# Layer 0's second FFN product by seven quarter products, with conditioning work and late norms placed elsewhere

## The chip, the cores and the metric

One core of one Trainium2 chip runs the whole program. The metric is the device time of one execution in microseconds, of the kernel before the median of three runs. TensorE (PE) multiplies; VectorE (DVE), ScalarE (ACT) and GpSimd (POOL) do the rest; SyncE (SP) issues the loads, in program order.

## What is computed

A decoder trunk of two layers for 512 tokens of width 1024, in float32. Layer 0 mixes tokens with a gated MLP in chunks of 128, layer 1 with attention over 16 heads whose logits carry a forget gate; each is followed by a SwiGLU FFN with 2816 hidden columns. Shift, scale and gate of every norm come from a conditioning vector `c`.

```python
mod = c_act @ ada_w[layer] + ada_b[layer]
sh_m, sc_m, g_m, sh_f, sc_f, g_f = jnp.split(mod, 6, axis=-1)
h = modulate(rms_norm(x, pre_mix_g[layer]), sh_m, sc_m)
y = gmlp_mixer(h, ...) if layer < N_A_LAYERS else fox_mixer(h, ...)
x = x + g_m[:, None, :] * rms_norm(y, post_mix_g[layer])
h = modulate(rms_norm(x, pre_ffn_g[layer]), sh_f, sc_f)
g, u = jnp.split(h @ w_gu, 2, axis=-1)
y = (jax.nn.silu(g) * u) @ w_down
x = x + g_f[:, None, :] * rms_norm(y, post_ffn_g[layer])
```

After layer 0 keys, values and forget gates are projected from `x` under a modulation of their own (kv). The mixer of layer 0 takes `z = gelu(h @ w_in)`, halves `u` and `v`, normalises `v`, multiplies it by `w_s` over each chunk and by `u`, and ends with `w_out`.

## The kernel before

Every product is made of three with operands split into a high part (`whi`, rounded by ACT) and a rest (`wlo`, by DVE): high by high, high by rest, rest by high (`moving`, L298 to L300; `prods`, L535; `prod`, L411 to L413). `load_split` (L109) loads a piece of weights of 128x1024 into one of three `raw` buffers and splits it; the loads stand on SP in program order, and each waits until its buffer is free.

The stages follow one another on PE: `v` and then `u` columns of `w_in` in eight chunks (`zchunk`), `w_s` and the first half of `w_out` for 16 groups (`spatial`, `ytrans`, `wout0`), the second half of `w_out` (`moving` with a tail of five held pieces), layer 0's gate and up products (`ffn`, 22 steps `m`), its second product `w_down`, then vf (value and forget-gate columns), k, q, attention, `w_o`, and layer 1's FFN. Four row blocks of 128 tokens, `n` = 0 to 3, have their own PSUM banks.

At a stage's end `boundary` takes each row block: `residual` (L333) sums squares on ACT (`sumsq`, L325), multiplies by the gate row (`y`, L341), adds to `x` (L347) and sums squares of the new `x`; `xrs` makes the reciprocal root; `prenorm_half` (L266) then scales two row blocks to `xr` (ACT, L263), transposes them on PE (`ps_x`, L275) and writes `hT` (L250 to L257, with `keep` copies at vf).

The conditioning vector's products are done on DVE in blocks: `ada_block` (L179) loads 128x1024 of `ada_w` and reduces it against `c` (L182). Closures for the blocks stand in a list `bg`, from which `run_bg` takes some at fixed places in the program; within the FFNs each uses the single buffer `rawb`, elsewhere one of the three `raw`. Behind the last block of a kind a `fin` finishes its columns or its gate row.

Layer 0's second product is `moving` over two column halves and 22 row pieces: 2 x 22 x 4 x 3 = 528 products of 128x512. Layer 1's is `down` (L360): Strassen-Winograd over the quarters of weights and hidden values, seven products for eight, 462. It needs sums of hidden quarters (`sums`, L556, POOL) and of weight quarters, which `weight_sums` (L489) makes on DVE during the gate/up stage and stores to a scratch `td` in HBM.

The order on each engine is set by a scheduler from the program's order and from priorities: `boundary` runs under `high_priority`, `issue_after` and `behind_norm` hold instructions behind others, and `pin` keeps attention's instructions in the written order. In attention `ORDER` (L53) is a string of tokens per head: `score` (L1100 to L1105: products, minimum on DVE, exponential on ACT), transposes, values, and between them fillers. `headnorm` gives k and q their norms: squares on ACT, reductions on DVE (L976), one reciprocal root (`rsqrt`, L139), multiplications.

## Time and profile before

| | |
|---|---|
| median of 3 runs | 1352.62 us (1349.98 to 1353.37) |
| the profiled execution | 1356.19 us, of which its span 1354.2 |
| mean granted TensorE clock | 0.995 |
| PE busy | 1319.9 us, 97% |
| DVE, ACT, POOL busy | 870.5, 580.4, 221.3 us |
| DMA | 221.08 MB, mean 163 GB/s |

A span is from the first instruction to the last. PE's products are pipelined, so its busy time is the time in which some product was under way; an idle time in brackets is a real stop. A row of a timeline names the engine, the line, what is written from what, and the wait before it with the engine that ended it.

### The profile page before, as it was taken

The page shows a single profiled execution, that of the slowest core. Times are in us where ns is not written, and L with a number is a line of the kernel's source. Part 1 is how long each engine was busy: PE and PEld are TensorE (multiplying, and loading weights), DVE is VectorE, ACT ScalarE, POOL GpSimd, SP SyncE. Part 2 cuts the span into 40 slices and gives each one's busy share as a digit, 9 for nine tenths or more (in the row PEclk, how much of TensorE's full clock was granted, in tenths as well). Part 3 has the DMA queues.
Part 4 walks back from the last instruction along what each step waited for, and adds up shares of the span by engine and source line. Part 5 has one row for each costly group of instructions (what it writes and reads, how often), then busy time and mean ns, then how long its engine had stood idle before and what let it go on. Part 6 is the DMA issues. An engine that isn't in the chain of part 4 may idle for free.

```text
span 1354.2 us, 17576 instructions
## 1 busy us (share of the span) xinstructions
PE 1319.9 (97%) x6376; PEld 1102.7 (81%) x6376; DVE 870.5 (64%) x1572; ACT 580.4 (43%) x995; POOL 221.3 (16%) x216
## 2 busy tenths in 40 slices
PE   7999999999999999999999998999999999999997
PEld 5888888779888888787889886887799888888886
DVE  6869858656455555554564766888675554536688
ACT  6524433345232223112562536887552222224665
POOL 0000000012111111000020405675021221212000
PEclk9999999999999999999999998999999999999999
DMA  9564446733666666674232331111336767665663
GB/s 368 187 225 133 132 125 203 267 105 125 204 214 188 192 197 203 207 257 125 87 119 78 95 106 47 38 35 33 109 110 207 253 207 259 197 199 173 199 191 129
DMA packets 71336, 221.08 MB, mean 163 GB/s; under 512 B 8657, under 2 KB 8913, under 8 KB 71250
## 3 DMA queue, kind: packets, MB, share of 16 engines
q1 hardware_dynamic: 70674, 218.92, 50.4%
q8 instruction: 50, 0.82, 0.3%
q10 hardware_dynamic: 576, 1.05, 0.2%
q14 instruction: 36, 0.29, 0.1%
HBM read 206.03 MB, written 13.65 MB: 162 GB/s over the span
## 4 chain that ended last, share of the span: by engine, by line
PE 64%; DMA 5%; DVE 5%; ACT 2%; issue 1%; DVEq 0%; ACTq 0%
PE acc L535 33%; PE acc L298 4%; PE acc L299 4%; PE acc L300 4%; DMA rawb<-in_ada_t 4%; PE acc L1048 3%; PE acc L1135 1%; PE acc L1259 1%; PE ps_x L412 1%; PE ps_x L411 1%; PE ps_x L413 1%; PE acc L1260 1%; PE acc L1261 1%; PE acc L412 1%; PE acc L411 1%
## 5 line engine op out<-in xcount | busy, mean ns | idle before, releaser
L535 PE MATMUL acc<-hT,whi 128*128 128x512 f32 (+1 forms) x1600 | 425.0, 364 | 0.0
L116 ACT ACTIVATE whi<-raw 128x1024 fp32r<-128x1024 f32 (+2 forms) x190 | 197.6, 1042 | 452.1 <-PE acc L535 169.1
L120 DVE TENSOR_TENSOR wlo<-raw,whi 128x1024 fp32r<-128x1024 f32 (+2 forms) x190 | 229.1, 1209 | 170.0 <-ACT whi L116 168.5
L535 PEld LDWEIGHTS acc<-hT,whi 128*128 128x128 f32 x1600 | 276.1, 189 | 47.4
L535 PE MATMUL acc<-hT,wlo 128*128 128x512 f32 (+1 forms) x800 | 263.6, 364 | 0.0
L535 PEld LDWEIGHTS acc<-hT,wlo 128*128 128x128 f32 x800 | 138.8, 189 | 23.7
L299 PE MATMUL acc<-wlo,hT 128*128 128x512 f32 (+1 forms) x352 | 135.0, 384 | 0.0
L300 PE MATMUL acc<-whi,hT 128*128 128x512 f32 (+1 forms) x352 | 134.8, 383 | 0.0
L298 PE MATMUL acc<-whi,hT 128*128 128x512 f32 (+1 forms) x352 | 134.5, 383 | 0.0
L182 DVE CUSTOM_DVE_ANT_0 rawb<-rawb,c_bc 128x1024 f32<-128x1024 f32 x59 | 77.1, 1307 | 83.9 <-DMA rawb<-in_ada_t 61.0
L299 PEld LDWEIGHTS acc<-wlo,hT 128*128 128x128 f32 x352 | 66.1, 188 | 12.7 <-DVE wlo L120 0.3
L298 PEld LDWEIGHTS acc<-whi,hT 128*128 128x128 f32 x352 | 66.1, 188 | 12.5
L300 PEld LDWEIGHTS acc<-whi,hT 128*128 128x128 f32 x352 | 66.1, 188 | 12.4
L257 POOL TENSOR_TENSOR hT<-hfull,hT 128x256 fp32r<-128x256 f32 x36 | 29.2, 819 | 277.7 <-DVE hT L256 154.8
L550 POOL TENSOR_TENSOR hid<-sg,hid 128x512 fp32r<-128x512 f32 (+1 forms) x25 | 36.7, 1471 | 193.5 <-ACT hid L549 193.5
L299 PE MATMUL acc<-wlo,hid 128*128 128x512 f32 x144 | 56.7, 394 | 4.5 <-DVE wlo L120 4.5
L182 DVE CUSTOM_DVE_ANT_0 raw<-raw,c_bc 128x1024 f32<-128x1024 f32 x37 | 45.1, 1220 | 20.8 <-DMA raw<-in_ada_t 20.6
L298 PE MATMUL acc<-whi,hid 128*128 128x512 f32 x144 | 56.1, 391 | 0.6 <-ACT junk L325 0.6
L300 PE MATMUL acc<-whi,hid 128*128 128x512 f32 x144 | 56.2, 390 | 0.0
L390 DVE TENSOR_TENSOR hT<-raw,hT 128x512 fp32r<-128x512 f32 x69 | 46.2, 702 | 13.1 <-ACT hT L389 12.9
L389 ACT ACTIVATE hT<-raw 128x512 fp32r<-128x512 f32 x69 | 42.0, 625 | 18.1 <-PE ps_x L412 7.1
L541 ACT ACTIVATE sg<-acc 128x512 f32<-128x512 f32 (+1 forms) x50 | 26.6, 536 | 52.1 <-PE acc L535 50.8
(336 smaller groups left out, 2370.0 us busy)
## 6 DMA issues: line engine op xcount, KB each, us to landing
raw<-in_w_gu SPq DMA_DIRECT2D x88, 512.0 KB
raw<-in_ada_t SPq DMA_DIRECT2D x53, 512.0 KB
raw<-in_w_down SPq DMA_DIRECT2D x44, 512.0 KB
rawb<-in_ada_t SPq DMA_DIRECT2D x43, 512.0 KB
raw<-in_w_in SPq DMA_DIRECT2D x32, 512.0 KB
raw<-td SPq DMA_DIRECT2D x44, 256.0 KB
raw<-in_w_down SPq DMA_DIRECT2D x33, 256.0 KB
raw<-in_w_out SPq DMA_DIRECT2D x16, 512.0 KB
```

Of the source, the lines that this page charges most:

```text
L116: ACT(hi[:, :width], raw[:, :width], AF.Copy)
L120: lo_eng.tensor_tensor(lo[:, :width], raw[:, :width], f32(hi[:, :width]), sub)
L182: nc.vector.tensor_tensor_reduce(raw, raw, c_bc, 1.0, 0.0, mul, add, dst)
L257: last = lo_eng.tensor_tensor(lo, full, f32(hi), sub)
L298: MM(banks[n], lh, wh, start=kt == 0, stop=False)
L299: MM(banks[n], lh, wl, start=False, stop=False)
L300: MM(banks[n], ll, wh, start=False, stop=kt == kts - 1)
L389: ACT(hi, w, AF.Copy)
L390: TT(lo, w, f32(hi), sub)
L535: MM(o, (hi, hi, lo)[z][:, ks], h[z == 1][kt][:, cs], start=i == 0, stop=i == 3 * KT - 1)
L550: nc.gpsimd.tensor_tensor(hid[1][m][:, cs], sg, f32(hid[0][m][:, cs]), sub)
L1048: pin(MM(box[0], (hi, hi, lo)[z][:, cs], h[z == 1][kt], start=kt + z == 0, stop=kt == KT - 1 and z == 2))
```

## The change

Layer 0's FFN takes the form of layer 1's: weight sums during its gate/up stage, `down` after it, the hidden values no longer split. `weight_sums` stores three pieces for four, and `down` makes the fourth, `t1`, again from the weights it loads; the store is put behind the next step. `down` has its own pool in both layers.

The blocks of `bg` are taken elsewhere: 12 in the last two `u` chunks, 14 in `wout0` (two for each pair of groups but the last), none before the second half of `w_out` and 6 (kv) in its tail, 28 in layer 0's gate/up stage (54 before), only a finish in its `down`, 24 in vf, k and q, where none stood before. The number of blocks is the same, 112 loads in all.

`lnorm` takes two operations for three. `prenorm_half` becomes a generator that transposes one row block, then the other; of a stage's second half it is held, and `next_late` lets it go on behind named products of the next stage. vf takes rows 2 and 3 first, which `down` finishes first. The reductions of the second half of q stand behind heads' scores (tokens B and C of head 0), its root and multiplications in pair 1.

```diff
-        for kp in range(KT // 2):
-            ps = aux.tile([P, 2, 256], F32, name="ps_x", tag="ps_s" if kp % 2 else "ps_t")
+        tr = [aux.tile([P, 2, 256], F32, name="ps_x", ...) for kp in range(KT // 2)]
+        yield
+        for kp in range(KT // 2):
+            turn(kp, 0)
+        yield
...
-        for i in range(NP):
-            r0 = halves(src[0, i, :, :512], td[i][:, 0])
-            r1 = halves(td[i][:, 1], td[i][:, 2])
+            b11, b12 = halves(src[0, i, :, :512], src[1, i, :, :512])
+            r1 = halves(td[i][:, 0], td[i][:, 1])
+            t1 = small.tile([P, S], F32, name="t1", tag="t2", bufs=3)
+            TT(t1, b12, b11, sub)
...
+                sums_at = dict(zip((4, 5, 7, 8, 10, 11, 13, 14, 16, 17, 19), range(NF // 2)))
...
-                                run_bg(1 if layer else 1 + j)
+                                run_bg(1 if layer or j == 0 or m % 3 == 0 or m > 15 else 0)
...
-                moving([w_down[layer, 0, i] for i in range(NF // 2)], NF, 512, lhs, first_half(y0, ss, row))
-                moving([w_down[layer, 1, i] for i in range(NF // 2)], NF, 512, lhs,
+                down(w_down[layer], td, qa, qb, fp, fd, row, done)
...
-                with tc.issue_after(ylast[0].ins):
-                    run_bg(2)
+                if g < 14:
+                    with tc.issue_after(ylast[0].ins):
+                        run_bg(2)
...
-               extra=lambda i: load_x(xp) if i == 2 else None)
+               extra=lambda i: load_x(xp) if i == 2 else None, n_bg=0, tail_bg=(3, 3, 0, 0))
...
-            for grp in ((0, 1), (2, 3)):
+            for grp in ((2, 3), (0, 1)):
...
+                        if kt == (3 if j else KT - 1):
+                            next_late(mm)
...
+                elif tok in "BC" and i == 0:
+                    for n in range(2 * "BC".index(tok), 2 * "BC".index(tok) + 2):
+                        later[n]()
+                elif tok == "C" and p_ == 1:
+                    close(0)
+                    later["end"]()
```

Three places in the order. First DVE at the end of w_out: `wlo` is a weight split (of w_out, then of gate/up weights), `y1` the first residual's product with the gate row. Before:

```order
L120 TENSOR_TENSOR wlo_2242<-raw_2238,whi_2240 128x1024
L120 TENSOR_TENSOR wlo_2622<-raw_2618,whi_2620 128x1024
L120 TENSOR_TENSOR wlo_2628<-raw_2624,whi_2626 128x1024
L341 TENSOR_TENSOR y1_2276<-acc_2118,grow_1600 128x512
L162 SCALAR_TENSOR_TENSOR rq_0_2279<-ss_565 128x1
```

Now (the rows that only read a block's sum out, 128x1, are left out):

```order
L120 TENSOR_TENSOR wlo_2253<-raw_2249,whi_2251 128x1024
L182 ISA raw_2255,A_kv_2121<-raw_2255,c_bc_75 128x1024
L182 ISA raw_2258,A_kv_2121<-raw_2258,c_bc_75 128x1024
L182 ISA raw_2261,A_kv_2121<-raw_2261,c_bc_75 128x1024
L182 ISA raw_2321,A_kv_2121<-raw_2321,c_bc_75 128x1024
L182 ISA raw_2324,A_kv_2121<-raw_2324,c_bc_75 128x1024
L182 ISA raw_2327,A_kv_2121<-raw_2327,c_bc_75 128x1024
L349 TENSOR_TENSOR y1_2296<-acc_2129,grow_1246 128x512
L162 SCALAR_TENSOR_TENSOR rq_0_2299<-ss_565 128x1
L120 TENSOR_TENSOR wlo_2608<-raw_2604,whi_2606 128x1024
L165 RECIPROCAL rpost_2297<-rq_1_2300 128x1
```

Six blocks stand between the last w_out split and the residual, and a gate/up split stands inside the residual's chain.

Second ACT at the change from the second FFN product to vf: the first `whi` of 128x704 in each list is vf's third piece, `x` the residual stream by row block (before, `x_2186` is block 2, and block 3 follows; now `x_2193` is block 0 and `x_2195` block 1, the last), `keep` and `hfull` belong to the prenorm. Before:

```order
L325 ACTIVATE junk,sx_2611<-x_2186 128x512
L163 ACTIVATE rq_5303<-rq_5302 128x1
L325 ACTIVATE junk,ss<-acc 128x512
L280 COPY keep_5186<-ps_x 128x2x256
L116 ACTIVATE whi<-raw 128x704
L163 ACTIVATE rq_5352<-rq_5351 128x1
L116 ACTIVATE whi<-raw 128x704
L263 ACTIVATE xr<-x_2186,rst_2610 128x1024
```

Now:

```order
L250 ACTIVATE hfull<-ps_x,B_kv,A_kv 128x256
L287 COPY keep_5636<-ps_x 128x2x256
L263 ACTIVATE xr<-x_2193,rst_2585 128x1024
L287 COPY keep_5637<-ps_x 128x2x256
L333 ACTIVATE junk,ss<-u_5138 128x512
L333 ACTIVATE junk,ss<-acc 128x512
L163 ACTIVATE rq_5787<-rq_5786 128x1
L333 ACTIVATE junk,sx_2586<-x_2195 128x512
L116 ACTIVATE whi<-raw 128x704
L333 ACTIVATE junk,sx_2586<-x_2195 128x512
L116 ACTIVATE whi<-raw 128x704
```

vf's third piece stood ahead of the last row block's residual; now it stands behind that residual, and behind the prenorm of the half that was finished first.

Third DVE at the start of attention: `mn` are score minima (`pr0` to `pr3` by row block; the first group is head 0's last, the other head 1's), `s8` the reductions of q, `rs` and `r8` the root. Before, with steps of the root left out:

```order
L1104 ISA pr3_6627,mn_6628<-ps_s_6624,mask_6289 128x512
L976 TENSOR_REDUCE s8_5919<-sqt_6637 128x8
L976 TENSOR_REDUCE s8_5919<-sqt_6647 128x8
L976 TENSOR_REDUCE s8_5919<-sqt_6657 128x8
L976 TENSOR_REDUCE s8_5919<-sqt_6667 128x8
L143 TENSOR_SCALAR rs_0_6671<-s8_5919 128x32
L146 TENSOR_SCALAR r8_5920<-rs_0_6671 128x32
L153 SCALAR_TENSOR_TENSOR rs_1_6672<-rs_1_6672,rs_0_6671 128x32
L154 SCALAR_TENSOR_TENSOR r8_5920<-rs_1_6672,r8_5920 128x32
L1104 ISA pr0_6697,mn_6698<-ps_s_6694,mask_6289 128x128
```

Now, with read-outs and four operations of the values' path left out:

```order
L1142 ISA pr0_7189,mn_7190<-ps_s_7186,mask_6781 128x128
L1142 ISA pr1_7196,mn_7197<-ps_s_7193,mask_6781 128x256
L1142 ISA pr2_7203,mn_7204<-ps_s_7200,mask_6781 128x384
L1142 ISA pr3_7213,mn_7214<-ps_s_7210,mask_6781 128x512
L1009 TENSOR_REDUCE s8_6387<-sqt_7147 128x8
L1009 TENSOR_REDUCE s8_6387<-sqt_7156 128x8
L1161 TENSOR_TENSOR pt3_1_6797<-ps_t_7219,pt3_0_6796 128x128
L1009 TENSOR_REDUCE s8_6387<-sqt_7165 128x8
L1009 TENSOR_REDUCE s8_6387<-sqt_7174 128x8
L1124 SCALAR_TENSOR_TENSOR k2_7269<-ps_z_7257,kqc_6380,k1_7267 64x512
L143 TENSOR_SCALAR rs_0_7474<-s8_6387 128x32
```

The reductions and the root stood ahead of head 1's minima; now the reductions stand behind them and the root later still.

## Rows read from the trace of the kernel before

**Rows 1.** The page: busy times, and VectorE's tenths in 40 slices of 33.9 us.

```profile
PE 1319.9 (97%) x6376; PEld 1102.7 (81%) x6376; DVE 870.5 (64%) x1572; ACT 580.4 (43%) x995; POOL 221.3 (16%) x216
DVE  6869858656455555554564766888675554536688
```

**Rows 2.** TensorE's waits: engine, line, awaited; us in total, times, longest.

```profile
PE ps_s L1100 <- DVE mn L1104: 6.7, 2, 5.4
PE acc L299 <- DVE wlo L120: 4.5, 4, 1.6
```

**Rows 3.** Timeline, TensorE in layer 1's `down`: start, length us, instruction, [idle before].

```profile
1240.72 0.39 PE L411 MATMUL acc<-hT,whi 128*128 128x512 f32 x1
1240.94 0.39 PE L412 MATMUL acc<-hT,whi 128*128 128x512 f32 x1
1338.34 0.50 PE L412 MATMUL acc<-wq,qh 128*128 128x512 f32 x1 [1.16 <-DVE wq L390]
```

**Rows 4.** The chain of waits in layer 0's `down`: start us, length us, what.

```profile
539.82 4.35 DMA rawb<-in_ada_t
550.98 1.23 DVE rawb L182
```

**Rows 5.** Timelines between w_out's halves: TensorE, then ScalarE.

```profile
255.45 0.39 PE L818 MATMUL acc<-whi,vl 128*128 128x512 f32 x1
257.18 0.49 PE L298 MATMUL acc<-whi,vh 128*128 128x512 f32 x1 [1.34 <-ACT junk L325]
262.81 0.40 PE L298 MATMUL acc<-whi,vh 128*128 128x512 f32 x1
255.49 1.06 ACT L116 ACTIVATE whi<-raw 128x1024 fp32r<-128x1024 f32 x1 [4.50 <-DMA raw<-in_w_out]
```

**Rows 6.** Timelines at the end of w_out: VectorE, ScalarE, TensorE.

```profile
275.67 1.23 DVE L120 TENSOR_TENSOR wlo<-raw,whi 128x1024 fp32r<-128x1024 f32 x1 [0.29 <-ACT whi L116]
283.69 0.69 DVE L341 TENSOR_TENSOR y<-acc,grow 128x512 f32<-128x512 f32 x1 [1.65 <-ACT junk L325]
290.61 1.14 ACT L263 ACTIVATE xr<-x,rst 128x1024 f32<-128x1024 f32 x1
291.87 0.60 PE L275 MATMUL ps_x<-ident,xr 128*128 128x128 f32 x4
309.64 0.66 PE L275 MATMUL ps_x<-ident,xr 128*128 128x128 f32 x4 [1.53 <-ACT xr L263]
```

**Rows 7.** Start of attention: timelines of VectorE and TensorE; busy times by stretch, PEclk.

```profile
822.80 1.69 DVE L143 TENSOR_SCALAR rs<-s 128x32 f32<-128x32 f32 x1
826.75 0.69 PE L1100 MATMUL ps_s<-k,q 128*128 128x384 f32 x1 [5.36 <-DVE mn L1104]
825.00:830.00 5.00, 3.25 (x10) 2.76 (x11) 2.90 (x14) 1.69 (x6) 3.37 (x4) 0.56 0.36 105
830.00:835.00 5.00, 5.00 (x26) 4.46 (x25) 2.04 (x6) 2.69 (x7) 0.68 (x1) 0.76 0.01 3
```

**Rows 8.** Start of vf: timelines of TensorE and VectorE, then one stretch.

```profile
679.71 0.32 PE L900 MATMUL acc<-whi,hT 128*128 128x352 f32 x1
685.51 0.66 PE L275 MATMUL ps_x<-ident,xr 128*128 128x128 f32 x4 [1.77 <-ACT xr L263]
693.10 1.53 PE L275 MATMUL ps_x<-ident,xr 128*128 128x128 f32 x12 [0.69 <-ACT xr L263]
686.21 1.42 DVE L347 SCALAR_TENSOR_TENSOR x<-y,rpost,x 128x512 f32<-128x512 f32 x2
694.70:700.50 5.80, 5.80 (x39) 5.80 (x38) 5.67 (x15) 5.80 (x13) 4.19 (x6) 1.00 0.22 62
```

**Rows 9.** Gate/up stages: weight-sum subtractions (layer 1); a stretch of layers 0 and 1.

```profile
L497 DVE TENSOR_TENSOR t<-raw 128x512 f32<-128x512 f32 x11 | 11.9, 1080 | 0.0
500.00:550.00 50.00, 50.00 (x222) 41.42 (x221) 29.21 (x37) 13.48 (x17) 6.52 (x5) 1.00 0.69 211
1060.00:1110.00 50.00, 50.00 (x222) 41.39 (x222) 23.22 (x30) 12.20 (x14) 9.06 (x8) 1.00 0.65 223
```

## Prediction before the run

> **What bounds the kernel now.** I read four views in order. The page's busy times come first: TensorE (PE) works 1319.9 of the 1354.2 us, VectorE (DVE) 64% [rows 1]. So the kernel gets faster only by fewer products or by closing PE's last 34 us of waits; another engine matters where PE waits for it. The list of PE's waits says where, with 6.7 us for the scores' minima and 4.5 for `wlo` among the longest [rows 2]. The timelines then place each wait, and the chain of waits shows what stands behind it. All numbers below are of the profiled execution, 1356.19 us, which is 3.6 above the median of 1352.62; I carry the difference over to the median.
>
> **The products.** A product of 128x512 starts 0.2267 us after the one before (1240.72, 1240.94) [rows 3]. Layer 0's second FFN product goes from 528 to 462: 66 fewer, 66 x 0.2267 = **-15.0 us**. Layer 1 already runs this form, and there PE waits once, 1.16 us for `wq` [rows 3]; I expect the same stop in layer 0: **+1.2**.
>
> **The conditioning blocks in layer 0's `down`.** Before, blocks still run there, each through one buffer `rawb`: a transfer of 4.35 us, then a reduction on DVE, 1.23 where nothing disturbs it [rows 4], one after the other. The weight split stands behind them on DVE, so PE waits for `wlo` four times, 4.5 us in all [rows 2]. After, no block is reduced there: **-5.0**, with some tenths for the slow first products. What takes DVE's time is the new form's own work; layer 1's stage shows PE waiting there only for `wq`, and only at its end.
>
> **The blocks that move.** Of blocks, 26 leave layer 0's gate/up stage (54 to 28), 1.3 us of DVE each with the read of the sum; 11 weight sums come in, four subtractions each, 1.08 us where POOL's sums run beside them [rows 9]: 47 us in, 34 out. That is 13 us more over 245, and DVE stands still in nearly half of that time (tenths of 5 [rows 1]). The sums add 11 loads of 1.05 MB and 11 stores of 0.79, less 26 blocks of 0.52 MB: 6.6 MB, 27 GB/s on top of 211; layer 1's same stage moves 223 GB/s, and both have PE busy 50.00 of 50.00 us [rows 9]. **0**, if that cover holds (last rival). Twelve blocks go to the last two `u` chunks, where DVE's tenths fall from 9 to 5 [rows 1], 24 to vf, k and q, where they are 4 to 7: 0; with the cover gone, a block costs at most its 1.23 us each. `lnorm` loses 16 DVE operations beside products: 0.
>
> **Between the two halves of w_out.** Before, SyncE issues the second half's first piece behind blocks; its `whi` starts at 255.49, the sums of squares that release the PSUM banks stand behind it on ScalarE (ACT), and PE stops 1.34 us [rows 5]. Then the clock drops: from 255.45 to 262.81 PE starts 16 products in 7.36 us where 16 x 0.2267 = 3.63 would do. After, three blocks and a finish are gone ahead of that load, which is issued earlier: **-3.7**.
>
> **At the end of w_out.** Six kv blocks now stand on DVE before the first residual. They pass the three-buffer ring in two rounds. The last `wlo` ends at 276.9 [rows 6]; a transfer of 3.6 (4.35 is the row's [rows 4]) and a reduction end the third block near 281.7, a second round the sixth near 286.5. Before, the residual's `y` started at 283.69 [rows 6]: 2.8 us late. Two gate/up weight splits follow inside the residual's chain, 1.2 each, one of them in its waits. The transposes stand 8 products later (1.8 us), and before, `xr` was done at 291.75 for transposes at 291.87 [rows 6]: no slack. So 2.8 + 1.2 - 1.8, about 2 us of a new wait; bounds 0 (loads that come sooner) and 5. The second half of the prenorm gains: its transposes waited 1.53 us [rows 6] and now come after 32 more products of 256 columns. I take 1.5. Together **+0.5**.
>
> **The start of attention.** Head 1's minima stood on DVE behind four reductions of q and a reciprocal root that begins at 822.80; PE stopped 5.36 us until 826.75, and the granted clock was 0.56 and 0.76 in the two stretches of 5 us from 825 [rows 7], 1.2 GHz in a part of each. PE worked 3.25 us of the first, at half speed, and 24% of the second is gone: 1.6 + 1.2 = 2.8. Together 8.2. After, the minima come first; I leave 0.9 for them, and 1 for the reductions that now disturb heads 0 and 1 to 3: **-6**, bounds -3.5 and -8.
>
> **The start of vf** is where the change costs. Groups now start with rows 2, 3, and the third piece's `whi` (the first of 128x704 in the second ACT list above) waits for the last residual, whose buffer it takes, behind the whole first prenorm half on both engines. Before, vf's first product started at 679.71 and the last residual `x` ended at 687.63: 7.9 us. The prenorm half adds what DVE did in its undisturbed stretch, 5.7 us [rows 8]. The split of 704 columns follows, 0.69 of the 1.06 and 1.23 us that 1024 take [rows 5, 6], 1.6: 15.2. Ahead of it PE has 24 products, 4.0 us before, and 16 transposes, of which 12 take 1.53 [rows 8]: 6. So it waits about 9, against 1.77 + 0.69 before: **+6.5**. Bounds: below, all of it is hidden, -2.5, since nothing excludes that the parts overlap; above, the prenorm half's 5.7 counts a second time, on ACT after DVE, +12. I take the middle, since the rows are those of this place.
>
> PE's clock after such a wait I take as unchanged, since it was after the 1.77 us one. The Trainium skill (TensorE: Matmul & The Clock Gate, Part 1: The HAM clock gate) says that an idle array falls to half its rate and that only sustained work releases it. The trace agrees after waits of 1.34 and 5.36 us [rows 5, 7], and does not after the one of 1.77 [rows 8]; by it the sum would lose another 2.8 us.
>
> **Sum:** -15.0 + 1.2 - 5.0 - 3.7 + 0.5 - 6 + 6.5 = -21.5: 1334.7 for an execution like the profiled one, **1331** for the median.
>
> **Rivals.**
> - *The vf boundary hides its chain.* For it: the residual's two last operations take only 1.42 us [rows 8], and the order gives PE transposes and products there. Against: the rows of this very place show the chain disturbed. Term -2.5 in place of +6.5: -30.5, 1322. Chance 0.2.
> - *The boundary is worse*: +12 there, 2.8 for the clock, 3 more at the end of w_out: -10.2, 1342. For it: three chains share ACT and DVE, and ACT's rows have no gap to give. Against: some work of the first chain is done before the last product. Chance 0.25.
> - *The change only moves attention's wait*: the scores' minima wait for the products themselves, and the reciprocal root stops a later head: 0 in place of -6, 1337. For it: DVE is busy over 80% of attention (tenths of 8 [rows 1]). Against: two pairs lie between. Chance 0.05.
> - *Slower: layer 0's gate/up stage starves.* The mechanism is SyncE's order: a weight sum's stores wait for its last subtraction, a block's load for the block before, and the gate/up load stands behind both. If each of the 11 sums makes PE wait one transfer of 3.5 us beyond its lead, that is 38 us: 1331 + 38 = 1369. It decides from 2.0 us a sum, where it eats the gain of 21.5. Against: layer 1 has the sums and 8 blocks with no wait of the gate/up products [rows 2, 9]; for it: layer 0 has 28 blocks. Chance 0.05.
>
> **How the numbers follow.** My forecast has 0.45: 1331, its own bounds 1326 to 1336. The range goes to 1318 (attention and w_out at their good ends with a hidden boundary) and to 1344 (the worse boundary, with both of its bounds); it leaves out the starved stage and little else. Within 0.3% (4 us, what a measurement tells from no change) means above 1348.6: only several mishaps together, 0.04. Slower 0.05, faster 0.91.
>
> **What would show it.** In the profile after: 66 fewer products, layer 0's `down` about 107 us long with one wait for `wq`; no wait at the first product of the second w_out half, and a granted clock of 1.00 there; a wait for `xr` of 2 us before the last products of w_out; at the first scores no wait over 1 us; at vf waits for `whi` or `wlo` of some 9 us. Wrong would be: a wait of gate/up products for `wlo` in layer 0, a clock below 1.00 after the vf wait, or a time above 1344 or below 1318.

## The result, and the profile after

| | before | after |
|---|---|---|
| median | 1352.99 us (4 runs) | 1361.86 us (4 runs, 1359.59 to 1363.41) |
| ratio to before, 95% interval | | 1.0063 [1.0045, 1.008] |
| profiled execution, its span | 1356.19, 1354.2 | 1363.41, 1361.4 |

The change made the kernel slower by 0.63%, about 8.5 us. The forecast was 1331, its range 1318 to 1344: a gain was forecast, a loss came.

The page of after, busy times, against [rows 1]:

```profile
PE 1309.3 (96%) x6310; PEld 1090.9 (80%) x6310; DVE 956.5 (70%) x1737; ACT 607.9 (45%) x1058; POOL 235.0 (17%) x235
```

The 66 products are gone (6376 to 6310), and PE's busy time fell by 10.6 us, less than 66 x 0.2267 = 15.0; products at half clock, of which there are more (below), count longer, which is a part of the difference. The span still grew by 7.2, so PE also stands still longer than before. DVE has 86 us more to do. PE's waits say where it stands (engine, line, awaited; us in total, times, longest), against [rows 2]:

```profile
PE acc L306 <- DVE wlo L120: 12.0, 7, 4.2
PE ps_x L275 <- ACT xr L263: 7.8, 3, 6.4
PE acc L915 <- ACT whi L116: 6.5, 1, 6.5
PE ps_s L1138 <- DVE mn L1142: 2.1, 3, 1.3
PE acc L419 <- DVE qa L551: 1.5, 1, 1.5
```

The minima's wait is down from 6.7 to 2.1, as forecast. But the weight splits of the streamed products (`wlo`, L306) now cost 12.0 us, the transposes at w_out's end 6.4, vf's third piece 6.5. The timelines of after place them (start, length in us, instruction, [idle before]), against [rows 5, 6, 8]:

```profile
262.58 0.39 PE L305 MATMUL acc<-whi,vh 128*128 128x512 f32 x1
...
281.29 1.23 DVE L182 CUSTOM_DVE_ANT_0 raw<-raw,c_bc 128x1024 f32<-128x1024 f32 x1 [0.20 <-DMA raw<-in_kv_ada_t]
...
283.84 1.23 DVE L182 CUSTOM_DVE_ANT_0 raw<-raw,c_bc 128x1024 f32<-128x1024 f32 x1 [1.32 <-DMA raw<-in_kv_ada_t]
...
292.69 1.22 DVE L182 CUSTOM_DVE_ANT_0 raw<-raw,c_bc 128x1024 f32<-128x1024 f32 x1 [1.91 <-DMA raw<-in_kv_ada_t]
...
293.84 0.68 DVE L349 TENSOR_TENSOR y<-acc,grow 128x512 f32<-128x512 f32 x1
...
303.42 1.33 PE L275 MATMUL ps_x<-ident,xr 128*128 128x128 f32 x5 [6.39 <-ACT xr L263]
...
683.08 0.75 DVE L355 SCALAR_TENSOR_TENSOR x<-u,rpost,x 128x512 f32<-128x512 f32 x1
...
683.89 0.77 ACT L116 ACTIVATE whi<-raw 128x704 fp32r<-128x704 f32 x1
...
684.72 0.95 PE L915 MATMUL acc<-whi,hT 128*128 128x352 f32 x2 [6.46 <-ACT whi L116]
...
725.67 1.23 DVE L182 CUSTOM_DVE_ANT_0 raw<-raw,c_bc 128x1024 f32<-128x1024 f32 x1 [2.51 <-DMA raw<-in_ada_t]
726.82 0.08 DVE L182 DVE_READ_ACCUMULATOR2_ANT A_f<- 128x1 f32 x1
726.82 0.87 DVE L120 TENSOR_TENSOR wlo<-raw,whi 128x688 fp32r<-128x688 f32 x1
...
727.75 0.65 PE L306 MATMUL acc<-wlo,hT 128*128 128x344 f32 x1 [4.17 <-DVE wlo L120]
```

The second w_out half starts with no stop (262.58). At w_out's end six reductions stand on DVE ahead of the residual's `y`, most of them with idle time before them in which DVE waits for that block's own load. In vf's last chunk the same happens at 725.67: DVE waits 2.51 us for the block's load and reduces 1.23, the split of the next piece, whose `whi` was done at 724.24, stands behind it, and PE waits 4.17 for that split. One row adds it up: the groups of DVE in vf, k and q of after, from 690 to 820 us (count | busy us, mean ns of one | idle just before, by whom ended):

```profile
L182 DVE CUSTOM_DVE_ANT_0 raw<-raw,c_bc 128x1024 f32<-128x1024 f32 x24 | 29.4, 1225 | 23.1 <-DMA raw<-in_ada_t 23.1
L120 DVE TENSOR_TENSOR wlo<-raw,whi 128x1024 fp32r<-128x1024 f32 (+1 forms) x22 | 26.5, 1211 | 5.0 <-ACT whi L116 5.0
```

The 24 blocks hold DVE's queue for 29.4 + 23.1 = 52.5 us of 130, 2.19 us each.

Stretches of after (PE, PEld, DVE, ACT, POOL busy; PEclk, DMA share, GB/s), against [rows 5, 7 to 9]:

```profile
255.00:265.00 10.00, 10.00 (x48) 8.27 (x47) 6.94 (x9) 4.99 (x11) 0.00 (x0) 1.00 0.89 305
...
825.00:830.00 5.00, 4.96 (x24) 4.02 (x23) 2.88 (x9) 2.12 (x6) 3.01 (x5) 1.00 0.36 105
...
400.00:550.00 150.00, 149.47 (x658) 122.90 (x657) 88.65 (x126) 37.09 (x43) 26.09 (x26) 1.00 0.77 260
...
700.00:820.00 120.00, 109.63 (x539) 94.33 (x538) 88.39 (x188) 43.72 (x67) 21.89 (x18) 0.99 0.58 180
```

The clock stays up between w_out's halves and at attention's start, and layer 0's gate/up stage keeps PE busy. From 700 to 820 PE lacks 10.4 us.

### The profile page after: what moved, and what is told of

Same layout as the page of the kernel before. It is cut to its first block, busy times and chain, and to the rows that moved or that the text cites. A ratio compares the mean times of both kernels' runs of the same rounds, so it can differ in the third digit from the quotient of the medians.

```text
span 1361.4 us, 17899 instructions
## 1 busy us (share of the span) xinstructions
PE 1309.3 (96%) x6310; PEld 1090.9 (80%) x6310; DVE 956.5 (70%) x1737; ACT 607.9 (45%) x1058; POOL 235.0 (17%) x235
## 5 line engine op out<-in xcount | busy, mean ns | idle before, releaser
L116 ACT ACTIVATE whi<-raw 128x1024 fp32r<-128x1024 f32 (+2 forms) x172 | 178.1, 1039 | 417.0 <-DMA raw<-in_w_gu 178.2
L120 DVE TENSOR_TENSOR wlo<-raw,whi 128x1024 fp32r<-128x1024 f32 (+2 forms) x172 | 212.2, 1237 | 102.2 <-ACT whi L116 101.4
L306 PE MATMUL acc<-wlo,hT 128*128 128x512 f32 (+1 forms) x352 | 136.6, 388 | 12.0 <-DVE wlo L120 12.0
L182 DVE CUSTOM_DVE_ANT_0 raw<-raw,c_bc 128x1024 f32<-128x1024 f32 x62 | 75.7, 1223 | 42.9 <-DMA raw<-in_ada_t 37.3
L306 PEld LDWEIGHTS acc<-wlo,hT 128*128 128x128 f32 x352 | 66.6, 189 | 27.2 <-DVE wlo L120 14.9
L398 DVE TENSOR_TENSOR hT<-raw,hT 128x512 fp32r<-128x512 f32 x116 | 79.2, 701 | 13.0 <-ACT hT L397 12.2
L397 ACT ACTIVATE hT<-raw 128x512 fp32r<-128x512 f32 x116 | 70.7, 624 | 23.4 <-DMA raw<-in_w_down 8.6
L182 DVE CUSTOM_DVE_ANT_0 rawb<-rawb,c_bc 128x1024 f32<-128x1024 f32 x34 | 41.5, 1221 | 54.9 <-DMA rawb<-in_ada_t 39.8
L557 POOL TENSOR_TENSOR qa<-qb,qa 128x256 f32<-128x256 f32 x22 | 27.4, 1244 | 212.1 <-DVE qa L551 212.1
L419 PE MATMUL acc<-hT,whi 128*128 128x512 f32 x144 | 56.1, 390 | 1.5 <-DVE qa L551 1.5
L421 PE MATMUL acc<-hT,wlo 128*128 128x512 f32 x144 | 56.4, 391 | 0.0
L420 PE MATMUL acc<-hT,whi 128*128 128x512 f32 x144 | 56.1, 389 | 0.0
```

The source lines that it names most:

```text
L116: ACT(hi[:, :width], raw[:, :width], AF.Copy)
L120: lo_eng.tensor_tensor(lo[:, :width], raw[:, :width], f32(hi[:, :width]), sub)
L182: nc.vector.tensor_tensor_reduce(raw, raw, c_bc, 1.0, 0.0, mul, add, dst)
L306: MM(banks[n], lh, wl, start=False, stop=False)
L397: ACT(hi, w, AF.Copy)
L398: TT(lo, w, f32(hi), sub)
```

## The experiments

The ratios are to the kernel before on the same chip; the last column is the ratio's difference to the changed kernel's 1.0063, times 1353 us.

| run | ratio [95%] | us against the change |
|---|---|---|
| e1, no blocks in vf, k, q | 0.9948 [0.9927, 0.997] | -15.6 |
| e2, none in u | 1.003 [1.0014, 1.0047] | -4.5 |
| e3, none at the end of w_out | 1.0011 [0.9996, 1.0025] | -7.0 |
| e4, all blocks as before | 1.0222 [1.0195, 1.0249] | +21.5 |
| e5, reductions one later | 1.0069 [1.0047, 1.009] | +0.8 |
| e6, own buffers | 1.009 [1.007, 1.011] | +3.7 |
| e7, both | 1.01 [1.0083, 1.0117] | +5.0 |
| e8, vf pieces in free buffers | 1.0041 [1.0021, 1.006] | -3.0 |
| e9, own buffers, order held | 1.0051 [1.0036, 1.0066] | -1.6 |
| e10, e9 and e8 | 1.0062 [1.0041, 1.0082] | -0.1 |
| e11, kv blocks into gate/up | 1.0077 [1.0057, 1.0097] | +1.9 |
| e12, kv blocks into w_out | 1.0064 [1.0049, 1.0079] | +0.1 |
| e13, loads by GpSimd | 1.0086 [1.0061, 1.0111] | +3.1 |
| e14, sums by GpSimd and ScalarE | 1.0123 [1.0102, 1.0144] | +8.1 |
| e15, the same in u and w_out | 1.0109 [1.0079, 1.0139] | +6.2 |
| d1, loads without reductions | 0.9998 [0.9986, 1.0011] | -8.8 |
| d2, reductions without loads | 1.0014 [0.9999, 1.0028] | -6.6 |
| f1, before and late q norms | 0.9964 [0.995, 0.9978] | |

The intervals reach 1.7 to 4.1 us to either side, and the changed kernel's own 2.4; its ratio was taken once and not again on each chip. So differences under some 4 us are weak alone, and there the text goes by the traces.

### Leaving the moved blocks out, place by place: e1, e2, e3

```diff
     def ada_block(src, dst):
+        if drop[0]:
+            nc.gpsimd.memset(dst, 0.0)
+            return
```

`drop[0]` is set in one of the three places.

> The changed kernel, with the 24 conditioning blocks of vf, k and q left out (their columns are set to zero, so layer 1's attention gate and FFN prenorm are computed from the biases alone); everything else stands. Theory A, the moved blocks are not hidden: each block's load takes a slot of the three-buffer ring behind a weight piece, and its reduction waits on DVE for that load with the next weight split queued behind it. Then the waits for wlo in vf's last chunk, in k and in q go (4.2 + 2.5 + 0.9 + 2.4 + 1.0 = 11.0 us, and about 0.7 of half clock): some -12 us against the changed kernel, about 1350. Rival B, the blocks lie beside products as the prediction had it, and this stretch lost its time at vf's start alone: 0 to -2 us, 1360 or more.

> The changed kernel with the 12 blocks of the last two u chunks left out (their columns are zero); everything else stands. Theory A: the waits in the u chunks go and the first half of w_out starts on a DVE that is not behind, so the drift of +2.7 at the end of u and of +4.2 more by the end of the first w_out half goes too: about -6.9 us, 1355. Rival B, the blocks are hidden and the drift comes from the two-step layer norm or from the later gate row: 0 to -1. Between them: only the drift inside u goes, -2.7.

> The changed kernel with the 6 kv blocks at the end of w_out left out (their columns are zero); everything else stands. Theory A: the first residual's y starts some 10 us earlier on DVE, the wait of 6.4 us for xr goes, and with it the half clock behind it (about 1.5 us): -8 us, 1354. Rival C: the wait comes from the new order of the transposes and of the prenorm's second half, which now stands behind gate/up products; then it stays, 0 to -1.

The same stretch as in the last row of after, in e1:

```profile
700.00:820.00 120.00, 119.96 (x605) 104.58 (x604) 68.03 (x150) 51.15 (x83) 25.13 (x24) 1.00 0.29 87
```

PE is full again, with 20 us less on DVE. Theory A held in all three places: -15.6, -4.5 (between the two prices named) and -7.0. They sum to -27.1, which would put the changed kernel at 1334.8; the three were not left out together. They show where the time went, not by what.

### The blocks back in their old places: e4

```diff
-                run_bg(1 if layer or j == 0 or m % 3 == 0 or m > 15 else 0)
+                run_bg(1 if layer else 1 + j)
```

and no `run_bg` in u, at w_out's end, in vf, k and q, as before.

> The seven-product form with all else of the change, but with every conditioning block where the kernel before has it: none in the u chunks, none at the end of w_out, 54 places in layer 0's gate/up stage, the rest in layer 0's second FFN product, none in vf, k and q. Theory A by the drifts of the two traces: 1361.9 - 12 (vf, k, q) - 6.9 (u) - 8 (end of w_out) + 3.7 (the stop between the w_out halves is back) + 5 (the waits in the second FFN product are back) = about 1344, 9 below the kernel before. Rival B, the boundaries and not the blocks lost the time: 1357 or more. Rival D, layer 0's gate/up stage cannot carry 54 blocks beside 11 weight sums: waits for wlo there, above 1350.

Slower by 21.5 than the change, as rival D had it; theory A had -18. PE's waits in e4 from 330 to 660 us:

```profile
PE acc L420 <- DVE hT L398: 11.2, 1, 11.2
PE acc L540 <- ACT whi L116: 5.2, 4, 2.8
PE ps_x L421 <- DVE wlo L413: 4.0, 1, 4.0
PE acc L540 <- DVE wlo L120: 2.9, 5, 0.8
```

Its stretch of the gate/up stage, beside the one of after above:

```profile
400.00:550.00 150.00, 141.91 (x610) 114.50 (x609) 93.10 (x136) 33.60 (x39) 23.68 (x24) 0.99 0.83 276
```

With 54 places beside the 11 weight sums, PE lacks 8.1 us of 150 there. But the larger loss stands behind that stage, which rival D did not name: layer 0's `down` begins with a wait of 11.2 and carries the blocks that are left. The groups of DVE in e4 from 560 to 709 us:

```profile
L182 DVE CUSTOM_DVE_ANT_0 rawb<-rawb,c_bc 128x1024 f32<-128x1024 f32 x25 | 30.6, 1224 | 17.1 <-DMA rawb<-in_ada_t 17.0
```

By the timelines, the time from `down`'s first product to vf's first is 148.7 us in e4 and 110.9 in after. So the blocks had to leave `down` above all, and a part of them the gate/up stage, for the seven products to pay. The first price of the sum, 0 for the stage with 28 blocks, stands; my price for moving the others does not.

### Why a block costs: buffers and order, e5 to e7 and e9

```diff
-        nc.vector.tensor_tensor_reduce(raw, raw, c_bc, 1.0, 0.0, mul, add, dst)
+        wait.append(lambda: nc.vector.tensor_tensor_reduce(raw, raw, c_bc, 1.0, 0.0, mul, add, dst))
+        flush(depth[0])
```

e5 sets `depth` to 1 in vf, k and q. e6 gives vf and k a pool of two buffers `rawb`; e7 does both.

> The changed kernel, all 24 blocks of vf, k and q kept and in the same ring, but each block's reduction is written one block later, so that it stands on DVE behind the next piece's split; the load stays where it was. What the 24 blocks cost in all is known from leaving them out: 14.6 us. Theory A1, DVE stands at a reduction whose own load has not landed, with the split behind it: most of it comes back, -9 to -14 against the changed kernel, 1348 to 1353. Rival A2, it is DVE's time of 24 x 1.25 = 30 us beside the norms and casts of k and q: 0 to -3. Rival A3, the ring's three slots are what runs out: a block now holds its slot longer, so 0 or slower by up to 5.

> The changed kernel with two buffers of their own for the blocks of vf and k (18 of the 24; those of q stay in the ring); each reduction stays right behind its load. Theory A1, DVE waits for the block's own load in front of the split: the wait stays, -2 to -5 since a load is issued sooner. Rival A3, blocks take the ring's slots from the pieces: -8 to -12. Rival A2, DVE's time: 0 to -3.

> Both at once for the blocks of vf and k: two buffers of their own, and each reduction one block later. Theory A1 and A3 alike: what 18 of 24 blocks cost comes back, -10 to -12 against the changed kernel, 1350 to 1352. Rival A2, DVE's time: 0 to -3.

e5 gave nothing: DVE's row still has 23.1 us of idle before the 24 reductions, and SyncE still issues a block's load only when a reduction has freed a slot (one ends at 718.31, the next load is issued at 718.33). e6 and e7 tested something else than meant, and no number expected of them came. The groups of DVE in e6 from 560 to 660 us, in layer 0's `down`:

```profile
L188 DVE CUSTOM_DVE_ANT_0 rawb<-rawb,c_bc 128x1024 f32<-128x1024 f32 x18 | 22.0, 1223 | 1.6 <-DMA rawb<-in_ada_t 1.6
```

Freed from the ring, all 18 were scheduled ahead into `down`, with hardly a wait for their loads. DVE is busy for 85 us of these 100 without them, and PE's busy time fell from 98.50 to 91.83. From `down`'s first product to vf's first e6 takes 126.5 us (after: 110.9), from there to the first scores 145.4 (after: 154.8): what the blocks no longer cost in vf and k, they cost, and more, in `down`. e9 holds loads and reductions to their written order with `keep_in_program_order`, all 24 in vf and k:

> The changed kernel, all 24 blocks kept: 10 in vf, 14 in k (two per piece for six pieces), none in q; two buffers of their own, each reduction one block later, and both the load and the reduction held to the order in which they are written, so that none can run ahead into layer 0's second FFN product as in the two runs before. DVE does the same 24 x 1.25 = 30 us. Theory A3, SyncE's queue and the ring's three slots are what runs out when blocks and pieces take turns in them: the waits for wlo go, -9 to -13 against the changed kernel, 1349 to 1353. Rival A2, DVE's time: 14 blocks in k are 17 us more of DVE in 44 us that are full of norms and casts, so -3 to +3.

```profile
L189 DVE CUSTOM_DVE_ANT_0 rawb<-rawb,c_bc 128x1024 f32<-128x1024 f32 x24 | 29.7, 1243 | 13.0 <-DMA rawb<-in_ada_t 12.9
```

DVE's waits for loads fell from 23.1 to 13.0, the time by 1.6 only. PE's waits in e9 from 690 to 830 us moved on:

```profile
PE acc L316 <- DVE wlo L120: 6.0, 3, 5.0
PE ps_t L1075 <- issue: 1.5, 1, 1.5
PE ps_t L987 <- DVE dk L982: 1.3, 1, 1.3
```

The -1.6 lies in rival A2's range (DVE's time), theory A3's -9 to -13 did not come: the waits for `wlo` fell from 10.3 to 6.0, and others came up, one of them for a small operation of DVE (`dk`).

### Another queue, other engines: e13, e14, e15

```diff
-        hold(nc.sync.dma_start(raw, src))
+        hold((nc.gpsimd if keep_order else nc.sync).dma_start(raw, src))
```

for e13, and for e14 (in vf and k) and e15 (in u and at w_out's end)

```diff
-        nc.vector.tensor_tensor_reduce(raw, raw, c_bc, 1.0, 0.0, mul, add, dst)
+        nc.gpsimd.tensor_tensor(raw, raw, c_bc, mul)
+        ACT(raw, raw, AF.Copy, accum_out=dst)
```

> The changed kernel with the 18 blocks of vf and k in two buffers of their own, reductions one later and held in written order on DVE (as in e9, but one per piece in k; the 6 of q stay in the ring), and their loads issued by GpSimd instead of SyncE. DVE's work is the same 24 x 1.25 = 30 us; SyncE's queue now holds only the pieces, so no piece's load stands behind a block's load that waits for a buffer. Theory Q, SyncE's order is what holds the pieces back: vf's last chunk and k run without waits for wlo, -8 to -11 against the changed kernel (about 1352), with q's 2.7 and 1.2 left. Rival A2, DVE: its queue, full of norms, casts and reductions, is what lets the splits go late; then waits for wlo remain in k and the gain is 0 to -4, like e9's -3.8.

> The same 18 blocks with their loads on SyncE again, and DVE taken out of them: GpSimd multiplies (128x1024) and ScalarE sums with its accumulator, one block later. SyncE's order stays as it was, the buffers are freed by GpSimd and ScalarE instead of DVE. Rival A2, DVE's time is the cause: -8 to -11 against the changed kernel (about 1352), with q's waits left. Theory Q, SyncE's order: 0 to -4. If GpSimd's multiplies slow DVE's two-operand work down, as its sums did beside the weight sums (1.08 us for 0.72), a part of the gain is lost: -4 to -6.

> The changed kernel with the 12 blocks of the last u chunks and the 6 at the end of w_out multiplied by GpSimd and summed by ScalarE, in the same ring and places; nothing else is moved. Leaving these blocks out gave 2.9 and 6.3 us. Rival A2, DVE is the cause (in u its splits, at the end of w_out the residual behind six reductions): -5 to -9, about 1354. Theory Q, their loads and slots: 0 to -2; or slower, where a multiply that takes GpSimd 2 to 3 us holds a slot longer than DVE's 1.25.

All three were slower than the change, e13 by 3.1, less than the noise. PE's waits in e13 from 690 to 830 us:

```profile
PE ps_t L1075 <- issue: 4.4, 1, 4.4
PE ps_s L968 <- DVE ls L960: 3.3, 1, 3.3
PE acc L316 <- DVE wlo L120: 2.8, 3, 1.4
```

The waits for `wlo` in vf, k and q fell to 2.8 us, as theory Q said, but 4.4 before the transpose of `selT` between k and q (no releaser shown) and 3.3 for the forget gate's `ls` on DVE took their place, and theory Q's gain of 8 to 11 did not come: SyncE's order alone is not the cause. In e14 the wait only changed its engine. The groups of GpSimd (whole run) and ScalarE (690 to 830 us):

```profile
L190 POOL TENSOR_TENSOR rawb<-rawb,c_bc 128x1024 f32<-128x1024 f32 x18 | 47.2, 2635 | 42.5 <-DMA rawb<-in_ada_t 34.1 <-ACT v L906 4.1 <-ACT whi L116 2.7
```

```profile
L191 ACT ACTIVATE rawb<-rawb 128x1024 f32<-128x1024 f32 x18 | 19.2, 1068 | 31.3 <-POOL rawb L190 31.3
```

ScalarE, which makes every `whi`, now stands 31.3 us waiting for GpSimd's multiplies, 2.64 us each against DVE's 1.23 for the whole reduction. In e15 ScalarE waits 40.2 us for 17 such multiplies. The first half of w_out starts 8.8 us later than in after (211.31 for 202.52), and the second half, with the blocks at its end, takes 54.1 us to the first gate/up product against 54.7 in after. Of what was expected only the last clause came, slower because a multiply holds a slot longer.

### Each half of a block alone: d1, d2

d1 keeps the loads and replaces the reduction; d2 reduces a standing tile and has no loads (18 of 24).

```diff
+        if light[0]:
+            nc.vector.tensor_copy(dst, raw[:, 0:1])
+            return
```

> The changed kernel; the 24 blocks of vf, k and q keep their loads, their slots in the ring and their place in SyncE's and DVE's order, but DVE only copies one column of each (so the columns of layer 1's gate and FFN prenorm are not the products they should be): 24 x 1.25 = 30 us of DVE are gone, and the slot is still freed by DVE. If DVE's time is what the blocks cost, this gives back what leaving them out did: about -13 against the changed kernel, 1349. If it is their loads, the ring and SyncE's order: 0 to -4.

> The other half: 18 of the 24 blocks (vf and k; the 6 of q stay whole) keep their reductions on DVE, in written order behind the piece's split, but read one standing tile, and their loads are left out (so the columns come out zero): DVE's 18 x 1.25 us stay, the ring, SyncE's queue and the DMA have the pieces alone there. If loads, ring and order are the cause: vf's and k's waits go, -7 to -10 against the changed kernel, 1352 to 1355, with q's 2.7 and 1.2 left. If DVE's time is: 0 to -4.

The stretch 700 to 820 us, first of d1, then of d2:

```profile
700.00:820.00 120.00, 118.23 (x593) 102.19 (x592) 68.04 (x174) 48.85 (x78) 23.60 (x23) 1.00 0.58 187
```

```profile
700.00:820.00 120.00, 115.54 (x568) 98.48 (x567) 90.89 (x189) 45.72 (x73) 23.00 (x20) 1.00 0.39 119
```

PE lacked 10.4 us of 120 in after, 1.8 without DVE's time (and the DMA at the same 0.58), 4.5 without 18 of the loads (and DVE at 90.9, more than in after). By the medians d1 gives back 8.8 us and d2, where q's six blocks stay whole, 6.6, against 15.6 for both. So neither theory alone was right: a block costs through both halves. How the loss splits is not settled, since the medians leave 6.8 us to the loads alone where the traced stretch leaves 1.8.

The waits for the loads are still there in d1. The groups of DVE from 690 to 820 us:

```profile
L185 DVE COPY A_f<-raw 128x1 f32<-128x1 f32 x8 | 1.2, 151 | 10.5 <-DMA raw<-in_ada_t 10.5
L185 DVE COPY g_m<-raw 128x1 f32<-128x1 f32 x8 | 1.2, 150 | 5.9 <-DMA raw<-in_ada_t 5.9
L185 DVE COPY B_f<-raw 128x1 f32<-128x1 f32 x8 | 1.1, 143 | 5.6 <-DMA raw<-in_ada_t 5.6
```

That is 22.0 us, against 23.1 in after, and PE hardly stands. Nor do such waits cost PE anything in layer 0's gate/up stage of after (317 to 562 us):

```profile
L182 DVE CUSTOM_DVE_ANT_0 rawb<-rawb,c_bc 128x1024 f32<-128x1024 f32 x26 | 31.7, 1221 | 42.4 <-DMA rawb<-in_ada_t 27.2 <-DMA rawb<-in_kv_ada_t 15.2
```

So a wait for a load is not a cost by itself. My reading is that it becomes one where DVE has no room left to catch up. From 700 to 820 us DVE was busy or waiting for a block's load for 109.7 us of 120 in after, 96.6 in d2 and 88.0 in d1. That fits PE's losses in these three, but in e9 it was 101.2 and PE lacked 9.7, so this sum alone does not set the price.

### vf's start and the end of w_out: e8, e10, e11, e12

e8 puts vf's third piece into a pool on the free side of memory and the fourth into small tiles:

```diff
+        if (j, i) == (0, 3):
+            held[j, i] = fourth(vf_src(j, i), w)
+            continue
+        pool, bufs, slot = (aw, 4, 704) if j else (aw2, 1, 704) if i == 2 else (wp, 2, 1024)
```

> The changed kernel with one edit at vf's start: the third and fourth piece of 128x704 get buffers that nothing before them still uses, so their split no longer waits for the last residual; the four pieces of the second column chunk stay where they were. Theory E, that buffer is the cause of PE's wait of 6.5 us and of the half clock behind it (0.83 in the 20 us from 680): the wait falls to 0 to 2 us and the time by 5 to 8, about 1355. Rival F, the wait only moves to the second chunk's first piece, whose split follows the same residual 48 products later, or ACT is late by itself: 0 to -3.

> The run before with the third and fourth vf piece in free buffers as well. In the run that had this edit alone PE's 6.5 us at vf's start went down to 1, but the blocks behind took 2 us of it back in waits for wlo. Theory A3 with E: without the ring's waits the whole of it shows, another -5 to -7: 1343 to 1347. Rival A2: 1355 to 1359.

PE's waits in e8 from 660 to 760 us:

```profile
PE acc L306 <- DVE wlo L120: 3.4, 3, 1.5
PE ps_x L275 <- ACT xr L263: 2.0, 1, 2.0
...
PE acc L932 <- ACT whi L116: 1.0, 1, 1.0
```

Theory E on the mechanism: 6.5 went to 1.0, and the clock from 680 to 700 rose from 0.83 to 1.00. In the trace the time from vf's first product to the first scores fell by 6.9 us (147.9 for 154.8), but the median only by 3.0. The ten runs spread from 1352.84 to 1364.98, and the profiled one is the fastest, so where the median lost the rest is not shown. e10 was to show it and did not test it: the wait of 6.5 us was back. Its two block buffers stand first in the free memory, which I take for the reason.

e11 and e12 move the six kv blocks from the end of w_out:

```diff
-   n_bg=0, tail_bg=(3, 3, 0, 0))
+   n_bg=(0, 3, 3))                      # e12; e11: n_bg=0 and
+   run_bg(1 if layer or j == 0 or m not in (5, 8) else 0)
```

> The changed kernel with the 6 kv blocks taken from the end of w_out and given to layer 0's gate/up stage, six places more there (34 for 28). Theory G, that stage carries 34 and the blocks at the end of w_out cost what leaving them out gave back: -6, 1356. Rival D, the stage is full beside the weight sums (with 54 places it lost some 14 us): each further block costs 14/26 = 0.5 us, so -3, and waits for wlo or whi show there.

> The changed kernel with the 6 kv blocks taken from the end of w_out and put on the second and third piece of its second half, three each, in the ring. DVE stands idle there for two fifths of the time. Theory A3, ring and SyncE's order: the wait of 6.4 us for xr goes, but the three blocks between two pieces hold the next piece's load back and PE waits for wlo, 3 to 6 us: -1 to -4 in sum. Rival A2, only DVE's time counts: -6.

In both the wait of 6.4 for `xr` went, in both it was paid elsewhere, and no gain that was expected came. e11 waits for `wlo` in the gate/up stage and, at `down`'s start, 2.6 us for `qa` and 1.9 for `hT`: the stage that carries 28 blocks does not carry 34. In e12 PE waits inside w_out's second half:

```profile
279.85 0.49 PE L305 MATMUL acc<-whi,vh 128*128 128x512 f32 x1 [1.31 <-ACT whi L116]
281.11 0.80 PE L306 MATMUL acc<-wlo,vh 128*128 128x512 f32 x1 [0.77 <-DVE wlo L120]
```

with a granted clock of 0.84 from 279 to 290. That is 2.1 us of waits and 1.7 of clock; the rest of the 7 us is not placed.

### One part of the change by itself: f1

The kernel before, with `headnorm` and the head loop's two branches of the change, nothing else:

```diff
+                elif tok in "BC" and i == 0:
+                    for n in range(2 * "BC".index(tok), 2 * "BC".index(tok) + 2):
+                        later[n]()
+                elif tok == "C" and p_ == 1:
+                    close(0)
+                    later["end"]()
```

> The kernel before with one part of the change alone: q's late norms moved into attention; the eight products and every block stay where before has them. By the two traces attention gained 5.7 us from that part: PE's wait of 5.4 us for head 1's minima goes, and part of the half clock behind it. Theory N, the part stands on its own: -4.5 to -6.5 against the kernel before, ratio 0.995 to 0.997, which would beat both kernels. Rival P, before has its reductions at another point, and without the blocks that delay q in the changed kernel the minima are late for other reasons: 0 to -2.

Theory N. 1347.51 us (11 runs), -4.9 against before, with an interval of -3.0 to -6.8: it beats both kernels. The stretch in which PE stood before, 5 us each:

```profile
820.00:825.00 5.00, 5.00 (x33) 4.33 (x32) 4.63 (x12) 4.04 (x12) 2.00 (x2) 1.00 0.38 104
825.00:830.00 5.00, 4.80 (x29) 3.83 (x27) 4.86 (x11) 3.63 (x8) 3.91 (x6) 1.00 0.02 5
```

In [rows 7] PE had 3.25 of the second stretch, at 0.56.

## Why the prediction was wrong, step by step

- **The products, and the blocks out of layer 0's `down`: right.** By the timelines, from `down`'s first product to vf's first, before took 128.5 us and after 110.9: -17.6, against -15.0 + 1.2 - 5.0 = -18.8. The stop in it was for `qa`, 1.5 us at the start, not for `wq` at the end; 1.8 us more (1.2 for `xr`, 0.6 for `hT`) stand right before vf's first product.
- **Gate/up with 28 blocks, 0: right.** PE had 149.47 of 150 us. e4 and e11 show how near the edge that was, and give the last rival its place: with 54 blocks the stage starves.
- **Between w_out's halves, -3.7: right in its mechanism.** No stop, clock 1.00. But the 12 blocks now taken earlier, in u, cost 4.5 there (e2). And 1.7 of the 3.7 were the half clock (0.70 from 257.18 to 262.80), which f1, with a stop of 1.09 us in the same place, does not have (1.00 from 255 to 265): a price read from one execution.
- **The start of attention, -6: right.** The waits and the half clock went; f1 has -4.9 for this part alone.
- **The start of vf, +6.5: right in its mechanism, near in size by luck.** The third piece's `whi` started 0.06 us after the last residual ended (683.89), and PE waited 6.46 where I had 9: the residual ended 10.4 us after vf's first product, not 7.9 + 5.7. The sentence after it failed: I took the clock as unchanged. From 684.70 to 690.00 the granted clock was 0.50, the level of 1.2 GHz: 2.6 us. The wait, put too long, and the clock, left out, cancel: 6.46 + 2.6 - 2.46 = 6.6 against 6.5. The Trainium skill (TensorE: Matmul & The Clock Gate, Part 1: The HAM clock gate) says that an idle array falls to half its rate; the trace agrees here, with 2.6 us where the prediction named 2.8 and left them out of its sum.
- **The end of w_out, +0.5: the step that put the sixth reduction near 286.5 failed.** It ended at 293.9; 5.4 us of that came with the stage, which began later by that much, the other 2.0 from DVE's waits before single reductions. PE waited 6.39 where I had 2, also because it came sooner: without the stop and the half clock of [rows 5] it reached the transposes 34.5 us after the stage's first product, where before it took 34.7 with eight products less. The clock was 0.50 for 4.4 us behind the wait (303.30 to 307.70). Leaving the six blocks out gave 7.0.
- **The moved blocks, 0: this is the step that failed.** The prediction took DVE's idle tenths as cover, and 1.23 us a block as the most if the cover fails. In the time of the run they cost 0.65 us each in vf, k and q (15.6 for 24), 0.37 in u and 1.17 at w_out's end: under 1.23, but not 0. The step asked whether DVE had idle time, not whether the load had landed when DVE's queue came to the reduction. In vf, k and q a block held that queue for 2.19 us, 1.23 of work and the rest waiting, with the next split behind it and the ring's next slot behind that. The three places cost 15.6, 4.5 and 7.0: 27.1 of the 30.9 us between forecast and result, of which the forecast had about 2 at w_out's end. DVE's tenths of 4 to 7 were true and did not show this, and the bound was never put into the range: 24 x 1.23 = 29.5 us.

The block's load could have been priced. A block's load was issued at 720.58 and its reduction began at 725.67, 5.1 us later. The Trainium skill (SBUF — State Buffer, The DMA setup-cost knee) gives a fixed 2 us and the bytes at 436 GB/s; for 512 KB that is an estimate of 3.2 us. The trace's 4.35 [rows 4] is longer, and decides.

**What stays open.** Both halves of a block cost in vf, k and q, by d1 and d2, but how much each costs alone is not settled, and in u and at w_out's end the halves were not tried. Why e9, with 10 us less of DVE's waiting, gained only 1.6 is not settled. No placing of the 42 blocks that hides them was found, and the change without them was only summed from three runs.

## What to carry to other kernels

Before a load-and-reduce step is put "into idle time", charge the engine's in-order queue with the wait for its load as well as its run, and the shared ring with its slot; then name what stands behind it, and ask whether the engine has room left to catch up. A stage's busy share says how much work fits, not whether a late operand will stop the work queued behind. When a change bundles gains with a re-placing of side work, run each gain alone: here the late norms, the only part that was put into the old kernel by itself, beat both kernels.

## What the runs showed of the hardware

- **The clock after a wait.** After PE's waits of 6.39, 6.46 and 4.17 us the granted clock was 0.50 (303.30 to 307.70), 0.50 (684.70 to 690.00) and 0.62 (727.50 to 732.00). After one of 2.35 us at 773.58 it stayed 1.00 (773 to 780). In the kernel before, a wait of 1.34 us was followed by half clock [rows 5] and one of 1.77 was not [rows 8]; in f1 one of 1.09 in the place of the 1.34 was not either. The length of the wait alone does not decide.
- **DVE beside GpSimd.** The split of 1024 columns takes 1.22 us, and 2.33 at 775.25, where GpSimd makes `hT` from two operands (3.58 us for two from 775.17). The Trainium skill (GPSIMD Engine Reference, 1. Specifications) says that the two share SBUF interfaces and contend when DVE reads two SBUF inputs; the trace agrees, and puts it at 1.9 times.
- **GpSimd as a helper.** Its multiply of 128x1024 takes 2.64 us where DVE multiplies and sums in 1.23; both kernels that moved this work off the busy DVE were slower than the change (e14 by 8.1, e15 by 6.2).
